# Two PSUM banks in one instruction: kept sums, residual additions and copies of a decoder trunk

## The chip, the cores and the metric

The kernel runs on one core of a Trainium2 chip. The core has a matmul engine (TensorE, PE in the profile), a vector engine (VectorE, DVE), an activation engine (ScalarE, ACT), a general engine (GpSimd, POOL) and a queue that issues transfers (SyncE, SP). Matmul results go to PSUM, eight banks of 512 float32 values in each of 128 partitions; VectorE and ScalarE read them from there. The metric is the device time of one execution in microseconds, as the median of several runs.

## The reference

A trunk of two layers works on 512 tokens of width 1024 in float32. Each layer is a half-step SwiGLU FFN, a token mixer and a second half-step FFN, each followed by a residual addition and a LayerNorm:

```
x = layer_norm(ALPHA * x + 0.5 * swiglu(x, w_gu, w_down), g, b)
x = layer_norm(ALPHA * x + mixer(x), g, b)
x = layer_norm(ALPHA * x + 0.5 * swiglu(x, w_gu, w_down), g, b)
swiglu(x) = (silu(x @ w_gate) * (x @ w_up)) @ w_down
```

The mixer of the first layer is block-sparse attention with eight heads, that of the second a causal pooling mixer. The hidden width of an FFN is 2816, so the four FFNs hold most of the matmul work.

## The kernel before

**Precision.** Every float32 operand is split into a rounded high part and the remainder (`split`, line 98): ScalarE copies the source into the rounded type, VectorE subtracts. A product is three matmuls that add into one bank (`mm3`, line 103: lines 105, 106 and 107).

**Seven products for eight.** The FFN's large products, and the value projection of the attention, are computed by a scheme of Strassen's kind: a 2 by 2 block product takes seven block products, numbered 1 to 7, instead of eight. Some products share an accumulator and go on adding into it: 1, 6, 7 and 4 add one after the other into one pair of banks, 2 into a second pair, 5 and 3 into that second pair after it has been read (`BANKS`, line 628). A product covers two row tiles, t=0 and t=1, one bank each, so its result lies in a pair of neighbouring banks. `products` (line 779) runs 24 matmuls; in the last step the three matmuls of t=0 come first, then the three of t=1.

**What reads a product.** After products 1, 6 and 5 `keep` (line 668) copies the partial sum to SBUF on ScalarE. After products 2, 7 and 3 `finish` (line 673) adds a kept sum to the accumulator on VectorE, then applies SiLU on ScalarE and multiplies on VectorE (`gate`, line 661). After product 4 the gate reads the accumulator directly. In the down projection `down_product` (line 810) adds each accumulator into the residual `ax` on VectorE (line 818). The attention's value projection has the same structure (`v_product`, line 928, with `keep`, `added` and `value`).

**Banks.** `bank(i, name)` (line 95) allocates a tile of one bank under the tag of bank i, so that a new tile on it waits for the readers of the old one. `SUMS` and `SECOND` (lines 633 and 634) say which pair a product uses; FFN 0 shifts all numbers by four. The outputs of `gate` are transposed on TensorE into one of two single banks in turn, and ScalarE copies them to `hT` (`to_features`, line 688); this happens after products 5 and 4.

**Order.** TensorE's order is that of the program. `order(eight)` (line 172) writes the products (i, jj) of an FFN out by hand, where jj numbers groups of hidden columns; jj = FF and FF + 1 stand for the two groups of the down projection. For FFNs 2, 3 and 5 (numbered with the mixers as phases 0 to 5) it begins

```
(1, 1), (2, 1), (1, 2), (5, 1), (6, 1), (7, 1), (3, 1), (4, 1), ...
```

and for FFN 0 with (1, 1), (2, 1), (6, 1), (5, 1), (7, 1), (3, 1), (1, 2), (4, 1). The later groups run 2, 6, 5, 7, 3, then 1 of the next group, then 4. The other engines' instructions are ordered at build time by a planner that simulates when each is ready; all waits are placed from the reads and writes of tiles. Weights stream through 20 slots of SBUF, are split on ScalarE and VectorE some units ahead of their use (`prepare`, line 263), and free their slots when TensorE has used them. Each product takes two units.

Of the kernel before, what the change touches and what calls it, by code (L numbers as in the profile page):

```python
# [25 lines left out]
F32 = mybir.dt.float32  # L26
F32R = mybir.dt.float32r
AF = mybir.ActivationFunctionType
ALU = mybir.AluOpType
# [3 lines left out]
P = 128  # L33
S = 512
D = 1024
FF = 2816
# [4 lines left out]
ALPHA = (2 * DEPTH) ** 0.25  # L41
# [42 lines left out]
def trunk(ctx, tc, x_in, xt, rel_bias, ln_g, ln_b, w_gu, w_gq, w_dq, w_down, w_v, a_in, a_out, b_in, b_group, b_scale, b_out, onehot, out):  # L84
    nc = tc.nc
# [6 lines left out]
    ps = enter(tc.tile_pool(name="ps", bufs=1, space=PSUM))  # L92
    dram = enter(tc.tile_pool(name="dram", bufs=1, space=bass.MemoryType.DRAM))

    def bank(i, name):
        return ps.tile([P, 512], F32, tag=f"b{i}", name=name)

    def split(hi, lo, src):

        nc.scalar.activation(hi, src, AF.Copy)  # L100
        return nc.vector.tensor_tensor(lo, src, hi.bitcast(F32), op=ALU.subtract)  # L101

    def mm3(acc, sh, sl, mh, ml, first, last, shared=False):

        nc.tensor.matmul(acc, sh, ml, start=first, stop=False, skip_group_check=shared)  # L105
        nc.tensor.matmul(acc, sh, mh, start=False, stop=False, skip_group_check=shared)  # L106
        nc.tensor.matmul(acc, sl, mh, start=False, stop=last, skip_group_check=shared)  # L107
# [189 lines left out]
    def weights():  # L297
        taken[0] += 1
        while len(parts) < taken[0]:
            load_needed()  # L300
            prepare()
        return parts[taken[0] - 1]

    def retire(count=1):

        retired[0] += count
        run_ahead()


    ax = glob.tile([P, NT, D], F32, name="ax")  # L310
# [317 lines left out]
    BANKS = {1: 0, 6: 0, 7: 0, 4: 0, 2: 1, 5: 1, 3: 1}  # L628
# [4 lines left out]
    SUMS = {1: 0, 2: 4, 3: 0, 4: 4, FF: 0, 5: 4, 0: 0, FF + 1: 4}  # L633
    SECOND, TURNED = 2, 6
# [3 lines left out]
    def ffn(n, x, dest):  # L638
        with tc.tile_pool(name=f"ffn{n}", bufs=1) as fp:
            hT = [fp.tile([P, GROUP, S], F32, name=f"hT{n}")]  # L640
            later, kept, waiting, turn = {}, {}, [], [0]
            eight = n == 0
# [3 lines left out]
            def banks(b, count, name):  # L646
                return [bank((b + 4 * eight) % 8 + t, f"{name}_{t}") for t in range(count)]
# [13 lines left out]
            def gate(out, g, u, sign):  # L661
                nc.scalar.activation(out, g, AF.Silu, scale=sign)  # L662
                return nc.vector.scalar_tensor_tensor(out, u, sign, out, op0=ALU.mult, op1=ALU.mult)

            def gated(name):
                return fp.tile([P, 2, 256], F32, tag="gated", bufs=3, name=f"gated{n}_{name}")

            def keep(i, jj, acc):
                kept[i, jj] = fp.tile([P, 2, S], F32, tag=f"kept{BANKS[i]}", bufs=2 - BANKS[i], name=f"kept{n}_{jj}_{i}")
                for t in range(2):  # L670
                    nc.scalar.activation(kept[i, jj][:, t], acc[t], AF.Copy)  # L671

            def finish(i, jj, acc):

                half, h, k, sign = DONE[i]
                out = gated(f"{jj}_{i}")
                if k is None:
                    for t in range(2):
                        ins = gate(out[:, t], acc[t][:, 0:256], acc[t][:, 256:512], sign)
                else:  # L680
                    k = kept.pop((k, jj))
                    for t in range(2):
                        nc.vector.tensor_tensor(k[:, t], k[:, t], acc[t], op=ALU.add)  # L683
                    ins = gate(out, k[:, :, 0:256], k[:, :, 256:512], sign)
                waiting.append((out, 4 * jj - 4 + 2 * half, h))
                return ins
# [90 lines left out]
            accs = {}  # L777

            def products(i, jj, b, amid=lambda q: None):

                if i in (1, 2, 5):
                    accs[jj, BANKS[i]] = banks(SECOND if i != 1 else SUMS[0] if eight and jj == FF + 1 else SUMS[jj], 2, f"d{n}_{jj}_{i}")
                acc = accs[jj, BANKS[i]]
                for q in range(2):
                    wh, wl = weights()
                    for k in range(2):
                        c = slice(k * 512, (k + 1) * 512)
                        for t in range(2):
                            o = b[:, :, 2 * q + k, t * P:(t + 1) * P]
                            mm3(acc[t], o[:, 0], o[:, 1], wh[:, c], wl[:, c], q == 0 and k == 0 and i in (1, 2, 5),  # L790
                                q == 1 and k == 1 and i in (2, 3, 4), True)
                    amid(q)
                return acc
# [16 lines left out]
            def down_product(i, g):  # L810


                acc = products(i, FF + g, hid[g].parts[i])
                for t0, d, sign in {1: ((0, 0, 1),), 2: ((0, 0, 1),), 6: ((2, 0, 1),), 5: ((2, 1, -1),), 7: ((2, 1, -1),),
                                    3: ((2, 0, 1),), 4: ((0, 1, -1),)}[i]:
                    for t in range(2):
                        r = ax[:, t0 + t, d * 512:(d + 1) * 512]
                        nc.vector.scalar_tensor_tensor(r, acc[t], 0.5 / ALPHA * sign, r, op0=ALU.mult, op1=ALU.add)  # L818
                if i in ((1, 2, 6, 5, 7) if g == 0 else (1, 2, 6, 5)):
                    next(operands)  # L820
                with tc.issue_after(hid[g].last.ins) if g == 0 and i in (2,) else ExitStack():
                    retire(2)

            for i, jj in ORDERS[not eight]:
# [11 lines left out]
                if n == 0 and (i, jj) in RESIDUAL:  # L836
                    with tc.issue_after(queued["load"].ins):
                        t = RESIDUAL.index((i, jj))
# [12 lines left out]
                if not eight and (i, jj) in ((1, 1), (2, 1)):  # L851
                    acc = products(i, jj, x.parts[i], head(i, jj))
                else:
                    acc = products(i, jj, x.parts[i])
                if i in (1, 6, 5):
                    keep(i, jj, acc)
                if i in DONE:
                    ins = finish(i, jj, acc)
# [35 lines left out]
    def attention(n, x, dest):  # L894
        held[0] = 4
        with tc.tile_pool(name="att", bufs=1) as ap:
            oT, qk, v, probs, pT = {}, {}, {}, {}, {}
# [8 lines left out]
            accs, kept = {}, {}  # L906

            def keep(i, acc):
                kept[i] = ap.tile([P, 2, 512], F32, tag=f"kept{i % 5}", name=f"vkept{i}")
                for t in range(2):  # L910
                    nc.scalar.activation(kept[i][:, t], acc[t], AF.Copy)

            def value(t, d, src, sign):
                hi, lo = v["hi"][:, t, d * 512:(d + 1) * 512], v["lo", t // 2][:, t % 2, d * 512:(d + 1) * 512]
                if sign == 1:
                    split(hi, lo, src)
                else:
                    nc.scalar.activation(hi, src, AF.Copy, scale=-1.0)
                    nc.vector.scalar_tensor_tensor(lo, src, -1.0, hi.bitcast(F32), op0=ALU.mult, op1=ALU.subtract)

            def added(i, acc):

                k = kept.pop(i)
                for t in range(2):
                    nc.vector.tensor_tensor(k[:, t], k[:, t], acc[t], op=ALU.add)
                return [k[:, t] for t in range(2)]

            def v_product(i):
                if i in (1, 2, 5):
                    accs[BANKS[i]] = [bank({1: 0, 2: 2, 5: 2}[i] + t, f"v{i}_{t}") for t in range(2)]  # L930
                acc = accs[BANKS[i]]
                for q in range(2):
                    wh, wl = weights()
                    for k in range(2):
                        c = slice(k * 512, (k + 1) * 512)
                        for t in range(2):
                            mm3(acc[t], *x.stationary(i, 2 * q + k, t), wh[:, c], wl[:, c], q == 0 and k == 0 and i in (1, 2, 5),
                                q == 1 and k == 1 and i in (2, 3, 4), True)
                if i == 2:
                    v["hi"] = lnp.tile([P, NT, D], F32R, tag="stage", name="vh")  # L940
                if i in (2, 7):
                    v["lo", len(v) - 1] = glob.tile([P, 2, D], F32R, tag="act", bufs=ACT, name=f"vl{len(v) - 1}")
                if i in (1, 6, 5):
                    keep(i, acc)
                else:
                    srcs = acc if i == 4 else added({2: 1, 7: 5, 3: 6}[i], acc)
                    t0, d, sign = {2: (0, 0, 1), 7: (2, 1, -1), 3: (2, 0, 1), 4: (0, 1, -1)}[i]
                    for t in range(2):
                        value(t0 + t, d, srcs[t], sign)
                with tc.issue_after(x.last.ins):  # L950
                    retire(2)

# [51 lines left out]
            for hp in range(H // 2):  # L1004
# [20 lines left out]
                else:  # L1025
                    for i in range(4):
                        acc = bank(i + 2 if hp == 1 and i < 2 else i % 2, f"qk{hp}_{i}")
                        a_block(x, acc, *blocks[i])
                        project(acc, *names[i])
                        if i == 1:  # L1030
                            ins = outputs(h - 2, 4 if hp == 1 else 0)
# [196 lines left out]
```

## Time and profile before

| | |
|---|---|
| median of 3 runs | 1667.8 us (1667.7 to 1668.12) |
| profiled execution, first to last instruction (span) | 1665.5 us |
| TensorE, matmuls | 1652.6 us busy, 99% |
| TensorE, weight loads | 1395.9 us, 84% |
| VectorE | 1340.2 us, 80%, 1766 instructions |
| ScalarE | 931.5 us, 56%, 1299 instructions |
| keeps, line 671 | 120 of one bank, 598 ns each |
| sums, line 683 | 120 of one bank, 680 ns each |
| residual additions, line 818 | 112 of one bank, 684 ns each |

The profile gives the profiled execution's time only as its span; 2.3 us lie between the span and the median. Matmuls overlap one another in the record: each shows 0.39 us, and they start 0.23 us apart. A row of waits reads "engine, tile, line <- engine, tile, line that it waited for: total us, times, longest". In a timeline, x2 joins two instructions that follow one another.

### The profile page before, as it was taken

To read this page: it belongs to the slowest core of one execution; us is meant where nothing else is said; L and a number is where in the kernel's file an instruction comes from. 1 tells how busy PE (TensorE), PEld (TensorE's weight loads), DVE (VectorE), ACT (ScalarE), POOL (GpSimd) and SP (SyncE) were. 2 spreads that over 40 slices of the span, in tenths; PEclk is the share of its full clock that TensorE was granted. 3 is DMA by queue.
4 is the path that set the end of the run, shared out by engine and by line. 5 is a ranking of instruction groups with operands and counts; after the bars stand their busy time and mean duration, and the time that the engine had idled before them with its cause. 6 is when DMAs were issued, how large, how long until landed. Compare 5 with 4: busy or idle time off the path is not lost.

```text
span 1665.5 us, 21722 instructions
## 1 busy us (share of the span) xinstructions
PE 1652.6 (99%) x8123; PEld 1395.9 (84%) x8123; DVE 1340.2 (80%) x1766; ACT 931.5 (56%) x1299; POOL 151.0 (9%) x196
## 2 busy tenths in 40 slices
PE   9999999999999999999999999999999999999997
PEld 8888888898888888888988888889898888888886
DVE  8778798798675888888868888888787698879696
ACT  6556556366445765555566655555453665656560
POOL 1101010000001011100010111100000201101000
PEclk9999999999999999999999999999999999999999
DMA  9778676805157488776685887666624878867641
GB/s 303 189 219 247 183 193 174 236 5 189 52 143 194 119 245 220 193 189 179 173 232 136 245 221 192 188 179 174 204 77 113 197 204 221 227 166 202 172 148 60
DMA packets 93579, 299.91 MB, mean 180 GB/s; under 512 B 9441, under 2 KB 22793, under 8 KB 93473
## 3 DMA queue, kind: packets, MB, share of 16 engines
q1 hardware_dynamic: 69600, 211.84, 37.0%
q0 software_dynamic: 23872, 86.68, 28.6%
q8 instruction: 64, 1.05, 0.2%
q14 instruction: 43, 0.34, 0.1%
HBM read 296.36 MB, written 4.74 MB: 181 GB/s over the span
## 4 chain that ended last, share of the span: by engine, by line
PE 98%; DVE 1%; ACT 0%; DMA 0%; SPq 0%; issue 0%; DVEq 0%; ACTq 0%
PE d L105 21%; PE d L107 21%; PE d L106 21%; PE acc L107 4%; PE acc L106 4%; PE acc L105 4%; PE ft L696 2%; PE qk L106 2%; PE qk L105 2%; PE qk L107 2%; PE gu L107 2%; PE gu L105 2%; PE gu L106 2%; PE tp L428 1%; PE u L106 1%; PE u L107 1%
## 5 line engine op out<-in xcount | busy, mean ns | idle before, releaser
L101 DVE TENSOR_TENSOR lo<-raw,hi 128x1024 fp32r<-128x1024 f32 (+1 forms) x476 | 572.1, 1216 | 121.2 <-ACT hi L100 95.9
L100 ACT ACTIVATE hi<-raw 128x1024 fp32r<-128x1024 f32 (+1 forms) x476 | 495.8, 1055 | 265.3 <-DVE lo L101 86.2
L105 PE MATMUL d<-lo,x 128*128 128x512 f32 x1080 | 423.8, 392 | 0.0
L107 PE MATMUL d<-hi,x 128*128 128x512 f32 x1080 | 420.9, 390 | 0.0
L106 PE MATMUL d<-hi,x 128*128 128x512 f32 x1080 | 420.4, 389 | 0.0
L105 PEld LDWEIGHTS d<-lo,x 128*128 128x128 f32 x1080 | 202.8, 188 | 43.1 <-ACT kept L671 1.3
L107 PEld LDWEIGHTS d<-hi,x 128*128 128x128 f32 x1080 | 202.7, 188 | 42.7
L106 PEld LDWEIGHTS d<-hi,x 128*128 128x128 f32 x1080 | 202.9, 188 | 40.9
L105 PE MATMUL d<-lo,xh 128*128 128x512 f32 x448 | 175.3, 391 | 0.0
L107 PE MATMUL d<-hi,xh 128*128 128x512 f32 x448 | 174.4, 389 | 0.0
L106 PE MATMUL d<-hi,xh 128*128 128x512 f32 x448 | 174.4, 389 | 0.0
L146 DVE TENSOR_TENSOR raw<-raw,raw 128x1024 f32<-128x1024 f32 x98 | 118.7, 1218 | 25.3 <-DMA raw<-in_ffn_w_dq 13.5
L253 POOL DMA_DIRECT2D raw<-in_ffn_w_gq x80 | 71.1, 893 | 684.6 <-DMA raw<-in_ffn_w_gq 171.3
L671 ACT ACTIVATE kept<-d 128x512 f32<-128x512 f32 x120 | 71.5, 598 | 68.3 <-PE d L107 65.4
L107 PEld LDWEIGHTS d<-hi,xh 128*128 128x128 f32 x448 | 84.1, 188 | 17.7
L106 PEld LDWEIGHTS d<-hi,xh 128*128 128x128 f32 x448 | 84.1, 188 | 17.2
L105 PEld LDWEIGHTS d<-lo,xh 128*128 128x128 f32 x448 | 84.1, 188 | 16.9
L818 DVE SCALAR_TENSOR_TENSOR ax<-d,ax 128x512 f32<-128x512 f32 x112 | 73.3, 684 | 14.4 <-PE d L107 14.3
L683 DVE TENSOR_TENSOR kept<-kept,d 128x512 f32<-128x512 f32 x120 | 78.1, 680 | 6.5 <-PE d L107 6.4
L662 ACT ACTIVATE gated<-kept 128x512 f32<-128x512 f32 x60 | 37.8, 630 | 72.9 <-DVE kept L683 72.2
L460 DVE SCALAR_TENSOR_TENSOR ax<-acc,ax 128x512 f32<-128x512 f32 x48 | 33.0, 687 | 52.8 <-PE acc L107 52.3
L105 PE MATMUL acc<-lo,h 128*128 128x512 f32 x192 | 75.2, 392 | 0.0
(199 smaller groups left out, 2664.4 us busy)
## 6 DMA issues: line engine op xcount, KB each, us to landing
raw<-in_ffn_w_gq SPq DMA_DIRECT2D x206, 512.0 KB, 4.8
raw<-in_ffn_w_gq POOLq DMA_DIRECT2D x80, 512.0 KB, 7.4
raw<-in_ffn_w_dq SPq DMA_DIRECT2D x80, 512.0 KB, 3.4
raw<-in_ffn_w_dq POOLq DMA_DIRECT2D x32, 512.0 KB, 6.4
raw<-in_ffn_w_down SPq DMA_DIRECT2D x24, 512.0 KB, 4.3
ax<-in_ln_b POOLq DMA_DIRECT2D x20, 512.0 KB, 8.4
raw<-in_ffn_w_gu SPq DMA_DIRECT2D x18, 512.0 KB, 4.7
raw<-in_a_w_in SPq DMA_DIRECT2D x16, 512.0 KB, 4.8
```

What stands on the lines that cost most here:

```text
L100: nc.scalar.activation(hi, src, AF.Copy)
L101: return nc.vector.tensor_tensor(lo, src, hi.bitcast(F32), op=ALU.subtract)
L105: nc.tensor.matmul(acc, sh, ml, start=first, stop=False, skip_group_check=shared)
L106: nc.tensor.matmul(acc, sh, mh, start=False, stop=False, skip_group_check=shared)
L107: nc.tensor.matmul(acc, sl, mh, start=False, stop=last, skip_group_check=shared)
L146: nc.vector.tensor_tensor(d, d, more, op=ALU.add)
L253: queued["acc"] = nc.gpsimd.dma_start(p.tile, p.plus, accum_op=ALU.add)
L662: nc.scalar.activation(out, g, AF.Silu, scale=sign)
L671: nc.scalar.activation(kept[i, jj][:, t], acc[t], AF.Copy)
L683: nc.vector.tensor_tensor(k[:, t], k[:, t], acc[t], op=ALU.add)
L696: nc.tensor.transpose(tp[:, c, t * P:(t + 1) * P], out[:, t, c * P:(c + 1) * P], ident)
L818: nc.vector.scalar_tensor_tensor(r, acc[t], 0.5 / ALPHA * sign, r, op0=ALU.mult, op1=ALU.add)
```

## The change

All eight banks become one tile, `banks8`. `bank(i, name)` returns a slice of it, and the new `bank_pair(i)` a slice of two neighbouring banks. `products` and `v_product` take their accumulators as such a pair; the matmuls still write one bank each, in the same order. Each loop over t=0 and t=1 that read the two banks with an instruction each becomes one instruction over both: the keeps, the sums of a kept part and an accumulator, the direct gate of product 4, the residual additions, and in the attention the keeps, the sums and the splits of the values.

```diff
+    banks8 = ps.tile([P, 8, 512], F32, name="banks8")
+
     def bank(i, name):
-        return ps.tile([P, 512], F32, tag=f"b{i}", name=name)
+        return banks8[:, i]
+
+    def bank_pair(i):
+        return banks8[:, i:i + 2]
...
             def keep(i, jj, acc):
                 kept[i, jj] = fp.tile([P, 2, S], F32, tag=f"kept{BANKS[i]}", bufs=2 - BANKS[i], name=f"kept{n}_{jj}_{i}")
-                for t in range(2):
-                    nc.scalar.activation(kept[i, jj][:, t], acc[t], AF.Copy)
+                nc.scalar.activation(kept[i, jj], acc, AF.Copy)
...
                 if k is None:
-                    for t in range(2):
-                        ins = gate(out[:, t], acc[t][:, 0:256], acc[t][:, 256:512], sign)
+                    ins = gate(out, acc[:, :, 0:256], acc[:, :, 256:512], sign)
                 else:
                     k = kept.pop((k, jj))
-                    for t in range(2):
-                        nc.vector.tensor_tensor(k[:, t], k[:, t], acc[t], op=ALU.add)
+                    nc.vector.tensor_tensor(k, k, acc, op=ALU.add)
...
-                    accs[jj, BANKS[i]] = banks(SECOND if i != 1 else SUMS[0] if eight and jj == FF + 1 else SUMS[jj], 2, f"d{n}_{jj}_{i}")
+                    accs[jj, BANKS[i]] = bank_pair(((SECOND if i != 1 else SUMS[0] if eight and jj == FF + 1 else SUMS[jj]) + 4 * eight) % 8)
...
-                    for t in range(2):
-                        r = ax[:, t0 + t, d * 512:(d + 1) * 512]
-                        nc.vector.scalar_tensor_tensor(r, acc[t], 0.5 / ALPHA * sign, r, op0=ALU.mult, op1=ALU.add)
+                    r = ax[:, t0:t0 + 2, d * 512:(d + 1) * 512]
+                    nc.vector.scalar_tensor_tensor(r, acc, 0.5 / ALPHA * sign, r, op0=ALU.mult, op1=ALU.add)
...
             def value(t, d, src, sign):
-                hi, lo = v["hi"][:, t, d * 512:(d + 1) * 512], v["lo", t // 2][:, t % 2, d * 512:(d + 1) * 512]
+                hi, lo = v["hi"][:, t:t + 2, d * 512:(d + 1) * 512], v["lo", t // 2][:, :, d * 512:(d + 1) * 512]
...
-                for t in range(2):
-                    nc.vector.tensor_tensor(k[:, t], k[:, t], acc[t], op=ALU.add)
-                return [k[:, t] for t in range(2)]
+                nc.vector.tensor_tensor(k, k, acc, op=ALU.add)
+                return k
...
-                    for t in range(2):
-                        value(t0 + t, d, srcs[t], sign)
+                    value(t0, d, srcs, sign)
```

More of the change, by code (lines that the diff above doesn't have):

```diff
@@ L789, in products @@
                             o = b[:, :, 2 * q + k, t * P:(t + 1) * P]
-                            mm3(acc[t], o[:, 0], o[:, 1], wh[:, c], wl[:, c], q == 0 and k == 0 and i in (1, 2, 5),
+                            mm3(acc[:, t], o[:, 0], o[:, 1], wh[:, c], wl[:, c], q == 0 and k == 0 and i in (1, 2, 5),
                                 q == 1 and k == 1 and i in (2, 3, 4), True)
@@ L909, in keep @@
                 kept[i] = ap.tile([P, 2, 512], F32, tag=f"kept{i % 5}", name=f"vkept{i}")
-                for t in range(2):
-                    nc.scalar.activation(kept[i][:, t], acc[t], AF.Copy)
+                nc.scalar.activation(kept[i], acc, AF.Copy)
             def value(t, d, src, sign):
-                hi, lo = v["hi"][:, t, d * 512:(d + 1) * 512], v["lo", t // 2][:, t % 2, d * 512:(d + 1) * 512]
+                hi, lo = v["hi"][:, t:t + 2, d * 512:(d + 1) * 512], v["lo", t // 2][:, :, d * 512:(d + 1) * 512]
                 if sign == 1:
@@ L923, in added @@
                 k = kept.pop(i)
-                for t in range(2):
-                    nc.vector.tensor_tensor(k[:, t], k[:, t], acc[t], op=ALU.add)
-                return [k[:, t] for t in range(2)]
+                nc.vector.tensor_tensor(k, k, acc, op=ALU.add)
+                return k
             def v_product(i):
                 if i in (1, 2, 5):
-                    accs[BANKS[i]] = [bank({1: 0, 2: 2, 5: 2}[i] + t, f"v{i}_{t}") for t in range(2)]
+                    accs[BANKS[i]] = bank_pair({1: 0, 2: 2, 5: 2}[i])
                 acc = accs[BANKS[i]]
@@ L936, in v_product @@
                         for t in range(2):
-                            mm3(acc[t], *x.stationary(i, 2 * q + k, t), wh[:, c], wl[:, c], q == 0 and k == 0 and i in (1, 2, 5),
+                            mm3(acc[:, t], *x.stationary(i, 2 * q + k, t), wh[:, c], wl[:, c], q == 0 and k == 0 and i in (1, 2, 5),
                                 q == 1 and k == 1 and i in (2, 3, 4), True)
@@ L947, in v_product @@
                     t0, d, sign = {2: (0, 0, 1), 7: (2, 1, -1), 3: (2, 0, 1), 4: (0, 1, -1)}[i]
-                    for t in range(2):
-                        value(t0 + t, d, srcs[t], sign)
+                    value(t0, d, srcs, sign)
                 with tc.issue_after(x.last.ins):
```

## The prediction

> **What bounds the kernel now.** I read the head of the page first, then the chain of waits, then the busy time of each engine by stage.
>
> ```profile
> span 1665.5 us, 21722 instructions
> PE 1652.6 (99%) x8123; PEld 1395.9 (84%) x8123; DVE 1340.2 (80%) x1766; ACT 931.5 (56%) x1299; POOL 151.0 (9%) x196
> PE 98%; DVE 1%; ACT 0%; DMA 0%; SPq 0%; issue 0%; DVEq 0%; ACTq 0%
> 0.00:10.50 10.50, 8.12 (x50) 7.50 (x50) 4.14 (x6) 5.91 (x7) 0.70 (x6) 1.00 0.79 288
> 1656.00:1666.00 10.00, 0.69 (x4) 0.22 (x2) 5.09 (x12) 0.20 (x1) 0.00 (x0) 0.68 0.28 107
> sum 1645.50, PE 1643.79 PEld 1388.15 DVE 1330.97 ACT 925.37 POOL 150.26; mean PE 328.76 PEld 277.63 DVE 266.19 ACT 185.07 POOL 30.05
> ```
>
> The first row of the two stages is the start-up, the second the tail (last residual add, LayerNorm, output). The sum row covers the five stages between, 10.5 to 1656 us. There TensorE is idle for 1645.50 − 1643.79 = 1.71 us in all. The rest of its idle time is start-up and tail, which the change does not touch. So VectorE's 80% and ScalarE's 56% bound nothing: relief for them is worth something only where TensorE waits for them. Those waits are listed by the weight loads, which run ahead of the matmuls and stop first:
>
> ```profile
> PEld ft L696 <- ACT hT L697: 1.6, 3, 0.5
> PEld d L105 <- ACT kept L671: 1.3, 3, 0.4
> PEld d L105 <- DVE raw L146: 0.9, 1, 0.9
> PEld o L105 <- DVE pr L971: 0.9, 1, 0.9
> PEld pt L983 <- DVE pr L975: 0.5, 1, 0.5
> PEld qk L105 <- DVE oT L101: 0.2, 1, 0.2
> ```
>
> Columns: total us, times, longest. Everything that could be won in the middle is 5.4 us, if all six rows went to nothing. Only the first two have an instruction of the change in or in front of them. They come three times each, once in each of the last three FFNs, so the question is what the change does at those two places.
>
> **The change part by part.** Prices of the instructions, from the groups with shapes kept apart:
>
> ```profile
> L671 ACT ACTIVATE kept<-d 128x512 f32<-128x512 f32 x120 | 71.5, 598 | 68.3 <-PE d L107 65.4
> L683 DVE TENSOR_TENSOR kept<-kept,d 128x512 f32<-128x512 f32 x120 | 78.1, 680 | 6.5 <-PE d L107 6.4
> L818 DVE SCALAR_TENSOR_TENSOR ax<-d,ax 128x512 f32<-128x512 f32 x112 | 73.3, 684 | 14.4 <-PE d L107 14.3
> L100 ACT ACTIVATE hi<-raw 128x1024 fp32r<-128x1024 f32 x474 | 494.5, 1057 | 264.4 <-DVE lo L101 86.2 <-PE d L105 62.9 <-PE d L107 43.0
> L100 ACT ACTIVATE pT<-pl 128x512 fp32r<-128x512 f32 x8 | 5.0, 631 | 5.7 <-DVE pl L1076 5.6
> L146 DVE TENSOR_TENSOR raw<-raw,raw 128x1024 f32<-128x1024 f32 x98 | 118.7, 1218 | 25.3 <-DMA raw<-in_ffn_w_dq 13.5 <-DMA raw<-in_ffn_w_gq 11.4
> ```
>
> The trace has no two-bank read. On ScalarE 512 more elements cost 1057 − 631 = 426 ns, so a pair copy is 598 + 426 = 1.02 us. Lower bound: 0.60 us, one bank's copy, if both banks streamed at once. Upper bound: 1.28 us, what two copies take together now (timeline below). I take 1.02, since the slope is from the same engine and operation at the same size. On VectorE the nearest 1024-element row is 1.22 us; two halves are 1.36.
>
> Busy time removed: ScalarE 60 × (2 × 0.598 − 1.02) = 10.4 us in the FFN keeps; VectorE 60 × (2 × 0.680 − 1.22) + 56 × (2 × 0.684 − 1.22) = 16.7 us in the sums and residual additions. The twenty direct gates and the attention's three keeps, three sums and four value splits shed an instruction per pair in the same way. All of it lies beside TensorE's work, so I cost the gain at nothing. No DMA is added, removed or moved in the program text.
>
> What the change adds is a later start. The first copy of a pair now starts when the t=0 group of matmuls is done, while the t=1 group runs. The pair copy waits for both, and both banks are given back at its end. The place where that hurts is product (6,1) followed at once by (7,1), which adds into the same two banks; `order(False)` puts them next to each other in FFNs 2, 3 and 5:
>
> ```profile
> 585.18 0.39 PE L107 MATMUL d<-hi,x 128*128 128x512 f32 x1
> 585.61 1.28 ACT L671 ACTIVATE kept<-d 128x512 f32<-128x512 f32 x2 [0.37 <-PE d L107]
> 585.87 0.39 PE L107 MATMUL d<-hi,x 128*128 128x512 f32 x1
> 586.26 0.19 PEld L105 LDWEIGHTS d<-lo,x 128*128 128x128 f32 x1 [0.43 <-ACT kept L671]
> 586.27 0.50 PE L105 MATMUL d<-lo,x 128*128 128x512 f32 x1
> 590.10 1.06 ACT L100 ACTIVATE x<-st 128x1024 fp32r<-128x1024 f32 x1 [3.20 <-DVE st L370]
> ```
>
> Now: t=0 ends at 585.18 + 0.39 = 585.57, its copy starts 0.04 later and ends at 585.61 + 0.60 = 586.21, and TensorE goes on at 586.26. After: t=1 ends at 586.26, the pair copy runs from 586.30 to 587.32, and TensorE goes on at 587.37. That is 0.04 + 1.02 + 0.05 = 1.11 us later than now, with bounds 0.69 and 1.37 by the two prices. Behind the waiting matmul stands the whole of TensorE's queue. ScalarE has nothing to put in between: its next work starts at 590.10. Three times: **+3.3 us** (2.1 to 4.1).
>
> The second place is the third group of transposes after (5,2), which needs the bank that the first `hT` copy empties; that copy stands behind the keep on ScalarE:
>
> ```profile
> 616.58 1.06 ACT L100 ACTIVATE hi<-raw 128x1024 fp32r<-128x1024 f32 x1 [0.72 <-PE d L105]
> 619.07 1.29 ACT L671 ACTIVATE kept<-d 128x512 f32<-128x512 f32 x2 [1.43 <-PE d L107]
> 619.33 0.40 PE L107 MATMUL d<-hi,x 128*128 128x512 f32 x1
> 620.26 1.08 ACT L697 ACTIVATE hT<-ft 128x512 f32<-128x512 f32 x2
> 620.90 0.42 PEld L696 LDWEIGHTS ft<-ident,gated 128*128 128x128 f32 x4 [0.54 <-ACT hT L697]
> ```
>
> Now the keeps end at 619.07 + 1.29 = 620.36. After, the pair starts at 619.33 + 0.40 + 0.04 = 619.77 and ends at 620.79: 0.43 later, and `hT` and the transposes with it (bounds 0 and 0.69). Three times: **+1.3 us** (0 to 2.1).
>
> Everywhere else a whole product lies between a pair's last matmul and the next one on its banks: 24 matmuls at (585.87 − 585.18) / 3 = 0.23 us, so 5.5 us. The pair ends 0.4 to 0.55 us later than the second half does now when the engine was waiting for it, and slightly earlier when the engine is behind. The tightest places now:
>
> ```profile
> 38.99 0.58 ACT L671 ACTIVATE kept<-d 128x512 f32<-128x512 f32 x1
> 41.47 0.39 PE L105 MATMUL d<-lo,x 128*128 128x512 f32 x1
> 599.80 1.27 DVE L683 TENSOR_TENSOR kept<-kept,d 128x512 f32<-128x512 f32 x2
> 603.10 0.48 PE L105 MATMUL d<-lo,x 128*128 128x512 f32 x1
> ```
>
> The first pair is the keep of (1,1) in FFN 0, done at 39.57 and needed at 41.47; the second the sum of (3,1) in FFN 2, done at 601.07 and needed at 603.10. Slacks of 1.9 and 2.0 us hide a half microsecond. If the cover went, each would cost what is left over it.
>
> Sum: 3.3 + 1.3 = 4.6 us (2.1 to 6.2). The span goes from 1665.5 to 1670.1. The profiled execution's span is 2.3 us under the median of the timed runs, 1667.8, which I take as what lies around the span; it stays. So 1672.4 us, with 1669.9 and 1674.0 from the bounds.
>
> The Trainium skill, Perfetto Trace Analysis, Optimizing Scalar/DVE Operations, says that grouping into larger operations helps where the engine is saturated, and that where Scalar and Vector are not saturated but leave bubbles on other engines, breaking instructions up may let work finish sooner. By its first half, with VectorE at 80% taken as saturated, the time would fall by at most the 5.4 us of waits; by its second half it rises as summed above. The rows of waits bear out the second.
>
> **The rivals.** *The planner fills the longer gap.* ScalarE idles 1.43 us before the keep of (5,2) and would idle 0.7 more. Weight slots come free twice a product, every 2.7 us; the copy at 616.58 waited for one, so the next could be ready at 619.3, before the pair. A copy of 1.06 us there ends at 620.36, the pair with the present overlap of 0.1 at about 621.3 instead of 620.79: 0.5 more, three times, 1673.9. For it: in FFN 0 the second copy of (1,1) at 38.99 already stands behind something else. Against: today the second keep, not such a copy, runs at that place.
>
> *Only the first wait grows.* If the planner sets the `hT` copies so that they do not stand behind the pair, the second place keeps its price: 1667.8 + 3.3 = 1671.1. Against: they are ready only after transposes that follow the product's last matmul, when the pair is ready already.
>
> *The other side: TensorE's own wait instructions.*
>
> ```profile
> L105 PEldq EVENT_SEMAPHORE  x74: 51/51/51, 4.8 to 1614.4; - x74
> L696 PEldq EVENT_SEMAPHORE  x43: 51/51/51, 48.3 to 1564.0; - x43
> ```
>
> TensorE's queue has 117 separate waits of 51 ns, 6.0 us. One tile and one reader per pair could make them needless. If they lay on the path and all went, the time would be 1667.8 − 6.0 + 4.6 = 1666.4; it decides only once more than three quarters go. Against: 6.0 us does not fit into 1.71 us of idle time, so most are hidden already.
>
> *The change does not do what it says*: each two-bank instruction is run bank by bank with its own wait, 1667.8. Nothing in the trace speaks for it. *One tile is waited for as a whole*: each of the 196 evacuations (60 + 60 + 20 + 56) holds TensorE about 1.1 us, 1667.8 + 216 = 1884. Against: the slices are of separate banks.
>
> **How the numbers follow.** Forecast 0.58, gap filled 0.12, only the first wait 0.14, wait instructions 0.06, no effect 0.07, whole tile 0.03. About 0.2%, 3.3 us, is what a measurement of this kernel can tell from no change. Of the forecast's 0.58 I put 0.11 under that bound, for its low price; of the second wait's rival 0.10 of 0.14, as 1671.1 is on the bound. Slower: 0.47 + 0.12 + 0.04 + 0.03 = 0.66. Faster: 0.03 of the wait instructions and 0.01 of no effect, 0.04. Same: 0.30. The range, 1667.5 to 1674.5, takes in both bounds, the first two rivals and no effect.
>
> **What would show it.** The keep should be 60 instructions of 128x1024 at about 1.02 us; the wait of L105 for the keep three times about 1.5 us instead of 0.43; the wait of L696 for `hT` three times about 0.97 instead of 0.54; TensorE's middle idle about 6.3 us instead of 1.7. ScalarE and VectorE should show less busy time and the time should not follow. A wait of TensorE at a third place, or a two-bank copy far from 1.02, would prove a step wrong; a median under 1667.8 all of it.

## The result, and the profile after

The changed kernel takes 1676.57 us (median of 5 runs, 1675.48 to 1676.7), beside 1667.78 us for the kernel before on the same chip: a ratio of 1.0051, 95% interval [1.004, 1.0063]. It is slower by 8.8 us. The forecast was 1672.4 us, 4.6 us more than before, with a range of 1667.5 to 1674.5. The profiled execution has a span of 1673.7 us, 8.2 us more than before.

The head of the page after, its chain of waits, the groups with shapes kept apart, and the stage between start-up and tail:

```profile
span 1673.7 us, 21430 instructions
PE 1654.1 (99%) x8123; PEld 1397.0 (83%) x8123; DVE 1328.2 (79%) x1623; ACT 922.7 (55%) x1212; POOL 150.8 (9%) x196
PE 94%; DVE 3%; ACT 2%; DMA 1%; issue 0%; SPq 0%; DVEq 0%; ACTq 0%
L675 ACT ACTIVATE kept<-banks 128x1024 f32<-128x1024 f32 x60 | 61.0, 1017 | 46.6 <-PE banks L112 46.5
L685 DVE TENSOR_TENSOR kept<-kept,banks 128x1024 f32<-128x1024 f32 x60 | 72.9, 1214 | 4.1 <-PE banks L112 4.1
L819 DVE SCALAR_TENSOR_TENSOR ax<-banks,ax 128x1024 f32<-128x1024 f32 x56 | 68.2, 1218 | 18.1 <-PE banks L112 17.2
10.50:1664.00 1653.50, 1644.16 (x8070) 1387.94 (x8071) 1318.81 (x1607) 916.81 (x1205) 150.10 (x190) 1.00 0.66 179
```

There are 292 instructions fewer (21722 before), VectorE is busy 12.0 us less and ScalarE 8.8 us less, and the time went up. TensorE's share of the chain fell from 98% to 94%: VectorE (3%) and ScalarE (2%) now stand in it. In the middle TensorE is idle for 1653.50 − 1644.16 = 9.3 us instead of 1.7. The weight loads' waits say where (total us, times, longest):

```profile
PEld banks L110 <- ACT kept L675: 4.6, 3, 1.5
PEld banks L698 <- ACT hT L699: 4.3, 3, 1.4
PEld banks L110 <- DVE lo L106: 2.6, 3, 0.9
```

Lines have moved by some: L110, L111 and L112 are the three matmuls that were L105 to L107, L105 and L106 the split that was L100 and L101, L675 the keep, L685 the sum, L698 and L699 the transposes and `hT`. The first two rows stood before with 1.3 and 1.6 us. The third is new. Each comes once in FFNs 2, 3 and 5; here they are in FFN 2.

**Place 1, (6,1) to (7,1)**, timeline after:

```profile
586.78 0.39 PE L112 MATMUL banks<-hi,x 128*128 128x512 f32 x1
587.20 1.02 ACT L675 ACTIVATE kept<-banks 128x1024 f32<-128x1024 f32 x1 [0.50 <-PE banks L112]
588.28 0.19 PEld L110 LDWEIGHTS banks<-lo,x 128*128 128x128 f32 x1 [1.54 <-ACT kept L675]
588.28 0.50 PE L110 MATMUL banks<-lo,x 128*128 128x512 f32 x1 [1.11 <-ACT kept L675]
```

From the last matmul of (6,1) to the first of (7,1), start to start, 588.28 − 586.78 = 1.50 us; before, 586.27 − 585.87 = 0.40. So +1.10 us, against 1.11 forecast.

**Place 2, the third transposes after (5,2)**, timeline after:

```profile
621.30 1.06 ACT L105 ACTIVATE hi<-raw 128x1024 fp32r<-128x1024 f32 x1 [3.01 <-PE banks L110]
621.33 0.40 PE L112 MATMUL banks<-hi,x 128*128 128x512 f32 x1
622.27 1.00 ACT L675 ACTIVATE kept<-banks 128x1024 f32<-128x1024 f32 x1
623.17 1.07 ACT L699 ACTIVATE hT<-banks 128x512 f32<-128x512 f32 x2
623.81 0.42 PEld L698 LDWEIGHTS banks<-ident,gated 128*128 128x128 f32 x4 [1.45 <-ACT hT L699]
```

The matmuls of (5,2) end at 621.33 + 0.40 = 621.73, and the pair could have started then. But ScalarE had begun another weight's split copy (its half of `split`, line 105 here) at 621.30, so the keep starts at 622.27 and `hT` behind it. The wait is 1.45 us instead of 0.54: +0.91, where 0.43 was forecast.

**Place 3, in the middle of a product, 8 us after the sum of (2,1)**. VectorE before, then VectorE and TensorE after:

```profile
568.86 1.30 DVE L683 TENSOR_TENSOR kept<-kept,d 128x512 f32<-128x512 f32 x2 [0.45 <-PE d L107]
570.08 1.22 DVE L101 TENSOR_TENSOR x<-st,x 128x1024 fp32r<-128x1024 f32 x1
571.21 1.22 DVE L101 TENSOR_TENSOR lo<-raw,hi 128x1024 fp32r<-128x1024 f32 x1
...
574.09 1.22 DVE L101 TENSOR_TENSOR lo<-raw,hi 128x1024 fp32r<-128x1024 f32 x1
```

```profile
569.52 1.22 DVE L106 TENSOR_TENSOR x<-st,x 128x1024 fp32r<-128x1024 f32 x1 [1.13 <-ACT x L105]
570.66 1.21 DVE L685 TENSOR_TENSOR kept<-kept,banks 128x1024 f32<-128x1024 f32 x1
571.79 1.22 DVE L375 SCALAR_TENSOR_TENSOR st<-st 128x1024 f32<-128x1024 f32 x1
572.93 1.22 DVE L106 TENSOR_TENSOR lo<-raw,hi 128x1024 fp32r<-128x1024 f32 x1
...
574.67 1.21 DVE L157 TENSOR_TENSOR raw<-raw,raw 128x1024 f32<-128x1024 f32 x1
575.81 1.22 DVE L106 TENSOR_TENSOR x<-st,x 128x1024 fp32r<-128x1024 f32 x1
576.94 2.35 DVE L106 TENSOR_TENSOR lo<-raw,hi 128x1024 fp32r<-128x1024 f32 x2
...
577.38 0.39 PE L112 MATMUL banks<-hi,x 128*128 128x512 f32 x1
578.21 0.50 PE L110 MATMUL banks<-lo,x 128*128 128x512 f32 x1 [0.45 <-DVE lo L106]
578.55 0.39 PE L111 MATMUL banks<-hi,x 128*128 128x512 f32 x1
```

Before, VectorE took the first half of the sum as soon as t=0 was done, then the second half, then the split of the operand `x`. After, the pair sum comes behind that split, and two more instructions (`raw` and the next `x`) have moved ahead of the second `lo`, which starts at 576.94 instead of 574.09. It is the remainder of a weight, done at 576.94 + 1.22 = 578.16, which TensorE needs at 577.38 + 0.23 = 577.61. From 577.38 to 578.21 are 0.83 us instead of 0.23, and the matmul after it is 0.11 late too: +0.71.

Per FFN 1.10 + 0.91 + 0.71 = 2.72 us; three times 8.2 us, the whole difference of the spans. The starts of the 8123 matmuls, set side by side in the two traces, drift apart at these nine places and by 0.2 us at the start-up; no other step exceeds 0.1 us.

### The profile page after: what moved, and what is told of

It is laid out like the page before. It is cut to its first block, busy times and chain, and to the rows that moved or that the text cites. A ratio compares the mean times of both kernels' runs of the same rounds, so it can differ in the third digit from the quotient of the medians.

```text
span 1673.7 us, 21430 instructions
## 1 busy us (share of the span) xinstructions
PE 1654.1 (99%) x8123; PEld 1397.0 (83%) x8123; DVE 1328.2 (79%) x1623; ACT 922.7 (55%) x1212; POOL 150.8 (9%) x196
## 4 chain that ended last, share of the span: by engine, by line
PE 94%; DVE 3%; ACT 2%; DMA 1%; issue 0%; SPq 0%; DVEq 0%; ACTq 0%
PE banks L110 30%; PE banks L112 30%; PE banks L111 30%; PE banks L698 2%; PE banks L433 1%; ACT st L441 1%; DVE lo L106 1%; ACT kept L675 1%; DVE x L106 0%; PE banks L981 0%; DVE st L375 0%; ACT x L105 0%; DMA raw<-in_ffn_w_gu 0%; ACT hi L105 0%; DVE kept L685 0%
## 5 line engine op out<-in xcount | busy, mean ns | idle before, releaser
L106 DVE TENSOR_TENSOR lo<-raw,hi 128x1024 fp32r<-128x1024 f32 (+1 forms) x476 | 570.4, 1216 | 130.3 <-ACT hi L105 101.2
L105 ACT ACTIVATE hi<-raw 128x1024 fp32r<-128x1024 f32 (+1 forms) x476 | 495.2, 1056 | 306.3 <-PE banks L110 103.0
L110 PE MATMUL banks<-lo,x 128*128 128x512 f32 x1136 | 446.0, 393 | 4.7 <-ACT kept L675 3.3
L112 PE MATMUL banks<-hi,x 128*128 128x512 f32 x1136 | 442.7, 390 | 0.0
L111 PE MATMUL banks<-hi,x 128*128 128x512 f32 x1136 | 442.2, 389 | 0.0
L110 PEld LDWEIGHTS banks<-lo,x 128*128 128x128 f32 x1136 | 213.3, 188 | 51.1 <-ACT kept L675 4.6
L112 PEld LDWEIGHTS banks<-hi,x 128*128 128x128 f32 x1136 | 213.2, 188 | 44.6
L111 PEld LDWEIGHTS banks<-hi,x 128*128 128x128 f32 x1136 | 213.4, 188 | 43.0
L110 PE MATMUL banks<-lo,xh 128*128 128x512 f32 x448 | 175.3, 391 | 0.0
L112 PE MATMUL banks<-hi,xh 128*128 128x512 f32 x448 | 174.4, 389 | 0.0
L111 PE MATMUL banks<-hi,xh 128*128 128x512 f32 x448 | 174.4, 389 | 0.0
L112 PE MATMUL banks<-x,lo 128*128 128x256 f32 (+1 forms) x424 | 133.8, 316 | 0.8 <-DVE lo L106 0.8
L110 PE MATMUL banks<-x,hi 128*128 128x256 f32 (+1 forms) x424 | 134.3, 317 | 0.0
L111 PE MATMUL banks<-x,hi 128*128 128x256 f32 (+1 forms) x424 | 133.6, 315 | 0.0
L112 PEld LDWEIGHTS banks<-hi,xh 128*128 128x128 f32 x448 | 84.1, 188 | 17.6
L110 PEld LDWEIGHTS banks<-lo,xh 128*128 128x128 f32 x448 | 84.1, 188 | 17.1
L111 PEld LDWEIGHTS banks<-hi,xh 128*128 128x128 f32 x448 | 84.2, 188 | 17.1
L675 ACT ACTIVATE kept<-banks 128x1024 f32<-128x1024 f32 x60 | 61.0, 1017 | 46.6 <-PE banks L112 46.5
L112 PEld LDWEIGHTS banks<-x,lo 128*128 128x128 f32 x424 | 80.8, 190 | 6.2 <-DVE lo L106 1.2
L110 PEld LDWEIGHTS banks<-x,hi 128*128 128x128 f32 x424 | 80.9, 191 | 5.5 <-DVE oT L106 0.2
```

The source lines that it names most:

```text
L675: nc.scalar.activation(kept[i, jj], acc, AF.Copy)
```

## The experiments

All times are beside runs of the kernel before on the same chip, whose median was 1667.51, 1667.69, 1667.5 and 1667.3 us in the four groups of runs below. This table is the result of all of them in one view. The columns in the middle are what the three places cost per FFN over the kernel before, read off the matmuls of FFN 2 in each run's trace as above (FFNs 3 and 5 agree within 0.1 us); "sum" is three times their total; the last columns are measured.

| run | place 1 | place 2 | place 3 | sum | measured | ratio to before, interval |
|---|---|---|---|---|---|---|
| the changed kernel | 1.10 | 0.91 | 0.71 | +8.2 | +8.8 | 1.0051 [1.004, 1.0063] |
| e1, one tile, all by bank | 0 | 0 | 0 | 0 | +0.2 | 1.0002 [0.9993, 1.0011] |
| e21, pair (6,1) alone | 1.10 | 0 | 0 | +3.3 | +3.2 | 1.0019 [1.001, 1.0029] |
| e22, pair (5,2) alone | 0 | 0.43 | 0 | +1.3 | +1.0 | 1.0008 [0.9998, 1.0017] |
| e32, pairs (6,1), (5,2) | 1.10 | 0.43 | 0 | +4.6 | +4.8 | 1.003 [1.0018, 1.0042] |
| e2, all keeps, nothing else | 1.10 | 0.91 | 0.29 | +6.9 | +6.5 | 1.0038 [1.0023, 1.0053] |
| e3, all but the keeps | 0.80 | 0 | 0 | +2.4 | +2.6 | 1.0015 [1.0005, 1.0025] |
| e4, all but keep (6,1) | 0.80 | 0.91 | 0.71 | +7.3 | +7.7 | 1.0046 [1.0031, 1.0061] |
| e13, all but keep (1,1) | 1.10 | 0.91 | 0 | +6.0 | +5.8 | 1.0034 [1.0021, 1.0047] |
| e25, keep (1,1) and the sums | 0.80 | 0 | 0.71 | +4.5 | +4.8 | 1.0031 [1.0019, 1.0042] |
| e23, pair (1,1) alone | 0.80 | 0 | 0.29 | +3.3 | +3.2 | 1.0019 [1.001, 1.0028] |
| e30, pairs (1,1), (6,1) | 1.10 | 0.74 | 0.29 | +6.4 | +6.0 | 1.0037 [1.0025, 1.005] |
| e31, pairs (1,1), (6,1), (5,2) | 1.10 | 0.91 | 0.29 | +6.9 | +6.5 | 1.0041 [1.0028, 1.0053] |
| e7, the changed kernel, order held at (5,2) | 1.10 | 0.43 | 0.71 | +6.7 | +6.8 | 1.0041 [1.0028, 1.0053] |
| e19, three keeps by bank, order held | 0.80 | 0 | 0 | +2.4 | +2.0 | 1.0013 [1.0004, 1.0022] |
| e20, e19 and another bank | 0.80 | −0.50 | 0 | +0.9 | +0.7 | 1.0006 [0.9997, 1.0015] |
| e9, kernel before and another bank | 0 | −0.50 | 0 | −1.5 | −1.1 | 0.9993 [0.9984, 1.0002] |

The sums stand within 0.6 us of every measurement. Nothing else in the change has a price that can be seen beyond that.

**The parts (e1, e2, e3).** e1 has the one tile and no pair at all; e2 pairs only the keeps of the FFNs; e3 pairs all but these.

```diff
 e1 (the keeps; sums, gates, residual additions and the attention likewise)
-                nc.scalar.activation(kept[i, jj], acc, AF.Copy)
+                for t in range(2):
+                    nc.scalar.activation(kept[i, jj][:, t], acc[:, t], AF.Copy)
 e2: as e1, with this line as in the changed kernel
 e3: the changed kernel, with these two lines
```

> The changed kernel with all its two-bank instructions taken apart again: only the one tile of eight banks is left. Theory (the later start of the pair copies costs all of it): 1667.8 us, within 0.5, with TensorE's waits as before the change (0.43 three times for the keep, 0.54 three times for hT). Rival (one tile makes the waits coarser): up to the changed kernel's 1675 to 1677.

> Of the two-bank instructions only the FFN's sixty keeps on ScalarE are left; sums, gates, residual additions and the attention go bank by bank. Theory (the keeps cost all): 1675.5 to 1676.6, with the three waits of the changed kernel, 1.53 for the keep, 1.45 for hT and 0.87 for a weight split, three times each. Rival (the pairs on VectorE cost part): below 1674, the wait for the weight split gone, 3.3 + 2.8 = 6.1 over the kernel before at most.

> The changed kernel with only the FFN's keeps taken apart again; all pairs on VectorE and in the attention stay. Theory: 1667.8 within 0.5, waits as before. Rival (pairs on VectorE cost part): 1669.9, with the 2.1 us of waits for the weight split left.

Measured 1667.68, 1674.0 and 1670.09 us. The tile itself costs nothing that can be measured: in e1 the two waits are those of the kernel before, within 0.1 us.

```profile
PEld banks L701 <- ACT hT L702: 1.6, 3, 0.5
PEld banks L110 <- ACT kept L676: 1.4, 4, 0.4
```

It also took away 40 of the 117 separate waits of TensorE that the prediction counted (74 and 43; now 70 and 7), and the time did not fall:

```profile
L110 PEldq EVENT_SEMAPHORE  x70: 51/51/51, 4.8 to 1614.5; - x70
L701 PEldq EVENT_SEMAPHORE  x7: 51/51/51, 48.3 to 1386.2; - x7
```

e2 landed between the two expectations: the keeps alone make most of the loss, but place 3 is smaller there (0.29), so the pairs on VectorE add to it (e25 below has 0.71 with the sums as pairs, e23 0.29 without). e3 was a miss: with every keep by bank nothing should have been lost, and 2.6 us were. Its ScalarE at place 1:

```profile
585.78 0.60 ACT L676 ACTIVATE kept<-banks 128x512 f32<-128x512 f32 x1 [0.94 <-PE banks L112]
586.28 1.05 ACT L105 ACTIVATE hi<-raw 128x1024 fp32r<-128x1024 f32 x1
587.23 0.59 ACT L676 ACTIVATE kept<-banks 128x512 f32<-128x512 f32 x1
```

and its waits:

```profile
PEld banks L110 <- ACT kept L676: 4.2, 6, 0.9
```

A split copy now stands between the two copies of (6,1), and TensorE waits six times instead of three. No pair is on ScalarE at this place. Pairs elsewhere had changed the order of its work.

**The two forecast terms by themselves (e21, e22, e32).** From e1, one or two keeps of FFNs 2, 3 and 5 are made a pair; the order at the three places stays that of the kernel before. VectorE's order is the same throughout; on ScalarE nothing moves in e22, and in e21 and e32 one split copy moves earlier by one place (at about 615 us in FFN 2), at no cost.

```diff
-                for t in range(2):
+                for t in (slice(0, 1), slice(1, 2)) if eight or (i, jj) not in ((6, 1), (5, 2)) else (slice(0, 2),):
                     nc.scalar.activation(kept[i, jj][:, t], acc[:, t], AF.Copy)
 e32 as shown; e21 with (6, 1) alone, e22 with (5, 2) alone
```

> One tile, everything bank by bank, but the keep of product (6,1) in FFNs 2, 3 and 5 as one pair copy. At this place the planner sets the other engines' instructions in the order of the kernel before. Theory (the later start alone costs 1.11 us here): the wait of L110 for the keep is about 1.53 three times, nothing else changes, 1667.6 + 3.3 = 1670.9. Rival (the later start is made up for elsewhere, and the first run's loss comes of the order alone): under 1669.2.

> One tile, everything bank by bank, but the keep of product (5,2) in FFNs 2, 3 and 5 as one pair copy; here too the planner leaves the order as before, with one split copy ahead of the keep and one behind hT. Theory (of the 0.92 us that the third transposes lost in the changed kernel, 0.43 are the pair's later end and the rest the second split copy that was set ahead of it): the wait for hT is 0.97, 1667.6 + 1.3 = 1668.9. Rival (the pair alone costs it all): wait 1.45, 1667.6 + 2.8 = 1670.4.

> One tile, everything by bank, and only the keeps of (6,1) and (5,2) in FFNs 2, 3 and 5 as pairs: six instructions fewer than by bank. VectorE's order after (2,1) and ScalarE's at (6,1) and (5,2) stay as before the change. Theory (the prediction's two terms hold where the order stays): waits of 1.5 and 0.97 us, three times each, 1667.7 + 3.3 + 1.3 = 1672.3. Rival (the two delays overlap, or the pair of (5,2) alone draws a split copy ahead): under 1671.3 or over 1673.3.

Measured 1670.85, 1668.69 and 1672.11 us. The waits of e32:

```profile
PEld banks L110 <- ACT kept L676: 4.6, 3, 1.5
PEld banks L701 <- ACT hT L702: 2.9, 3, 1.0
```

These are the forecast's waits of 1.5 and 0.97 us, and 1672.11 is 0.3 us from the forecast's time, 1672.4. Its two terms were right, singly and together, as long as the order of the other engines stays. (e22 alone can't be told from no change by its interval; its wait can.)

**Undoing one pair, or adding others (e4, e13, e25).**

```diff
 e4
-                nc.scalar.activation(kept[i, jj], acc, AF.Copy)
+                for t in (slice(0, 1), slice(1, 2)) if not eight and (i, jj) == (6, 1) else (slice(0, 2),):
+                    nc.scalar.activation(kept[i, jj][:, t], acc[:, t], AF.Copy)
 e13: the same with (1, 1)
 e25: e1 with the keep of (1, 1) a pair, and the sums of the FFNs as in the changed kernel
```

> The changed kernel with one keep taken apart, that of product (6,1) in FFNs 2, 3 and 5. Theory (each of the three places has its own price): the wait of L110 for the keep falls from 1.53 to 0.43, the other two stay, 3.3 us under the changed kernel, 1672.2 to 1673.3. Rival (what is lost at one place is won back or lost at the next): less than 1.5 us under the changed kernel.

> The changed kernel with one keep taken apart, that of product (1,1) in FFNs 2, 3 and 5; the sum of (2,1) stays a pair. Theory (that keep starts the reordering on VectorE): the wait for a weight split, 0.87 three times, is gone, the other two stay, 2.1 us under the changed kernel, about 1673.8. Rival (the pair sum on VectorE does it by itself): the wait stays, 1675.5 to 1676.6.

> One tile, bank by bank, but the keep of product (1,1) in FFNs 2, 3 and 5 and all sums on VectorE as pairs. The planner sets VectorE's work after (2,1) as in the changed kernel: the split of an operand ahead of the sum, the weight splits behind. Theory (third place: keep of (1,1) and sum of (2,1) together): the wait of L110 for a weight split comes back, 0.87 three times, 2.1 us; a split copy between the two copies of (6,1) costs another 2.0 as in the kernel with the keeps by bank; 1671.7 in all. Rival (the third place needs another pair): no wait for a weight split, 1669.6.

Measured 1675.19, 1673.53 and 1672.49 us. e4 missed: the pair of (6,1) was undone, but the split copy of e3 slipped between its two copies, and 0.80 of the 1.10 us stayed. e13 was right: without the pair of (1,1) place 3 is gone. e25 brought it back in full, with no other keep paired.

**Order alone (e23, e30, e31).** (1,1) is a keep for which TensorE waits in no run, so by the prediction it is free. It is the only pair of e23. e30 adds (6,1), e31 (5,2) too.

```diff
-                for t in range(2):
+                for t in (slice(0, 1), slice(1, 2)) if eight or (i, jj) not in ((1, 1), (6, 1)) else (slice(0, 2),):
 e30 as shown; e31 with (5, 2) as well, e23 with (1, 1) alone
```

> Only the keep of (1,1) as a pair, for which TensorE never waits. In the program as built an operand split stands between the two sums after (2,1), and a split copy between the two copies of (6,1). Theory (order alone costs): 0.8 us three times at (6,1) and 0.2 after (2,1), 2.4 + 0.6 = 3.0, so 1670.7. Rival (a pair whose banks are not needed soon is hidden, as the prediction had it): 1667.7.

> Only the keeps of (1,1) and (6,1) as pairs, that of (5,2) by bank. In the program as built a split copy stands between the two copies of (5,2). Theory (the order, not the pair at the place, makes the second place dearer): the hT copies stand behind first copy, split copy and second copy, about 0.74 us later than before, so 3.3 + 2.2 + 0.6 after (2,1) = 6.1 over the kernel before, 1673.8. Rival (without the pair of (5,2) the wait for hT stays 0.54): 1671.6.

> As the run before this one, with the keep of (1,1) a pair as well: three of 60 kinds of keep, nine instructions fewer. In the program as built a split copy stands ahead of the pair of (5,2), and an operand split between the two sums after (2,1). Theory: 3.3 + 3 x 0.92 at (5,2) + about 0.6 after (2,1) = 6.7 over the kernel before, 1674.4, as with all 60 keeps paired. Rival (the other 51 keeps matter too): 1672.3 to 1673.

Measured 1670.52, 1673.35 and 1673.78 us: 3.2, 6.0 and 6.5 us over the kernel before, where the theory had 3.0, 6.1 and 6.7. VectorE in e23:

```profile
569.18 0.69 DVE L688 TENSOR_TENSOR kept<-kept,banks 128x512 f32<-128x512 f32 x1 [0.64 <-PE banks L112]
569.79 1.22 DVE L106 TENSOR_TENSOR x<-st,x 128x1024 fp32r<-128x1024 f32 x1
570.92 0.68 DVE L688 TENSOR_TENSOR kept<-kept,banks 128x512 f32<-128x512 f32 x1
```

One pair on ScalarE, some 6 us earlier, and the operand split has gone between the two halves of the sum. That moves the weights' remainders at place 3, and a split copy at place 1: 3.2 us, none of it a wait for the pair. In e30 the keep of (5,2) is by bank as before the change, and place 2 is dearer all the same:

```profile
620.29 0.60 ACT L676 ACTIVATE kept<-banks 128x512 f32<-128x512 f32 x1 [2.16 <-PE banks L112]
620.78 1.05 ACT L105 ACTIVATE hi<-raw 128x1024 fp32r<-128x1024 f32 x1
621.73 0.59 ACT L676 ACTIVATE kept<-banks 128x512 f32<-128x512 f32 x1
622.21 1.09 ACT L702 ACTIVATE hT<-banks 128x512 f32<-128x512 f32 x2
```

and the wait for `hT`, 3.8 / 3 = 1.27 us against 0.54 before:

```profile
PEld banks L701 <- ACT hT L702: 3.8, 3, 1.3
```

Three pairs in each of FFNs 2, 3 and 5 (e31) cost what all sixty keeps cost (e2).

**Holding the order, and another bank (e7, e19, e20, e9).** e7 is the changed kernel with the second split copy after (5,2) issued behind the pair. e19 takes the three keeps by bank and holds the split copies behind them; e20 and e9 give the third transposes after (5,2) bank 0, e20 on top of e19, e9 on the kernel before. (`copied` is the keep's instruction. The three keeps by bank are 9 instructions more, 18 in all.)

```diff
 e7
+                elif not eight and (i, jj) == (5, 2):
+                    retire()
+                    with tc.issue_after(copied.ins):
+                        retire()
 e19: the same, the keeps of (1, 1), (6, 1) and (5, 2) by bank, and
-                        with tc.issue_after(x.last.ins):
+                        with tc.issue_after(x.last.ins), tc.issue_after(copied.ins) if i == 6 else ExitStack():
 e9, e20
+                    third = not eight and i == 5 and len(waiting) == 0 and jj == 2
-                    tp = banks(TURNED + turn[0] % 2, 1, f"ft{n}_{f}_{h}")[0].rearrange("p (c s) -> p c s", c=2)
+                    tp = banks(0 if third else TURNED + turn[0] % 2, 1, f"ft{n}_{f}_{h}")[0].rearrange("p (c s) -> p c s", c=2)
```

> The changed kernel with one ordering added: after product (5,2) in FFNs 2, 3 and 5 the second split copy of the next weights is issued behind the pair's keep instead of ahead of it. Nothing else differs. Theory (of the second place's price, 0.92 us against 0.43 forecast, 0.5 comes from that copy standing ahead of the pair): the wait for hT falls from 1.46 to 0.97 us three times, so 1.5 us less than the changed kernel, about 1675.1 against 1676.6. Rival (the transposes are late for another reason): no change, 1676.6.

> The changed kernel with the keeps of products (1,1), (5,2) and (6,1) in FFNs 2, 3 and 5 taken by bank again (two instructions each, 18 more in all), and with the split copies that the planner had let overtake them held behind the second copy of (6,1) and of (5,2). The other 51 keeps, all sums, gates and residual additions stay in pairs. Theory (the loss is those three places and the order around them, and pairs cost nothing elsewhere): no wait longer than before the change, 1667.8. Rival (pairs also cost by something that no wait shows, or the planner reorders at yet another place): 1669 or more.

> The kernel of the run before this one (three keeps by bank, copies held behind them, pairs elsewhere), and the third transposes after (5,2) in bank 0. Theory: 1667.8 less the 0.54 us of that wait three times, 1666.2, level with the kernel before with the third bank alone; pairs add no gain of their own, since nothing waits for VectorE or ScalarE elsewhere. Rival (the 20 us less busy time of the two engines are worth something once the waits are gone): under 1665.5.

> The kernel before with one edit: the third group of transposes after product (5,2) in FFNs 2, 3 and 5 uses bank 0, which has been read at that point, instead of the bank that the first hT copy still empties. Theory (the 0.54 us wait for hT is wholly a wait for that bank): it goes, 3 x 0.54 = 1.6 us, so 1666.2 and a ratio of 0.999 to the kernel before. Rival (bank 0 is needed again soon, or the transposes or the next product wait for something else as late): 1667.7, no change.

Measured 1674.33, 1669.52, 1668.16 and 1666.39 us. In e7 ScalarE waits for the matmuls and takes the pair first:

```profile
621.95 1.02 ACT L675 ACTIVATE kept<-banks 128x1024 f32<-128x1024 f32 x1 [3.48 <-PE banks L112]
622.87 1.08 ACT L699 ACTIVATE hT<-banks 128x512 f32<-128x512 f32 x2
```

Its wait for `hT`:

```profile
PEld banks L698 <- ACT hT L699: 2.9, 3, 1.0
```

The wait falls from 1.45 to 0.97 us (2.9 / 3), so the copy ahead was the other half of place 2's price. e19 missed by 2 us: place 2 and place 3 are free, but at (6,1) a split copy still runs between the two copies, as in e3. The order that I added holds only the copies issued after (6,1) in the program, and this is not one of them: in e1 ScalarE ran it ahead of both. e20 sits on the same 0.80. In e9 the wait for `hT` is gone from the list (TensorE is 0.50 us earlier behind it) and 1.1 us of the time; its interval reaches to 1.0002, so it can't be told from the kernel before. None of these kernels clearly beats it.

## Why the prediction was right or wrong

- **Nothing to win: right.** VectorE and ScalarE lost 20.8 us of busy time and TensorE got none of it. No effect falls by the sign, whole-tile waits (+216 us) by the size. TensorE's own wait instructions fall by e1: 40 of the 117 are gone there, and the ratio is 1.0002 [0.9993, 1.0011]; the other 77 stayed, so what they would give is not shown.
- **Prices: right.** The pair copy took 1.017 us (1.02 forecast), the sum 1.214 and the residual addition 1.218 (1.22). VectorE saved 12.0 us instead of 16.7 and more, because two halves that follow one another overlap in the record (1.30 us for two, not 1.36). ScalarE's keeps saved 71.5 − 61.0 = 10.5 us; the forecast's own terms give 10.6, not the 10.4 that it states. Nothing hung on either.
- **Place 1: right**, 1.10 against 1.11, by itself in e21. "ScalarE has nothing to put in between" held here, but not in general: in e3, e4, e19, e20, e23 and e25 a split copy runs between the two copies, for 0.80 us.
- **Place 2: mis-sized**, 0.91 against 0.43. The 0.43 is right where the order stays (e22, e32). The rest is the rival "the planner fills the longer gap": 0.5 more, as it was priced, at the place it named. I gave it 0.12, because "today the second keep, not such a copy, runs at that place". That was the old order, taken as evidence for the new one. Nor does the longer gap bring the copy there: e22 has the same pair and not the copy, e30 the copy and not the pair. The pairs of (1,1) and (6,1) were enough for it in e30; in the changed kernel the second of them is copied at 587.20 us, 34 us before the split copy at 621.30.
- **"Everywhere else … slacks of 1.9 and 2.0 us hide a half microsecond": the step that failed.** It asked only when the banks come back, and for that the slack does hide it. It left the order of ScalarE and VectorE as it was, as a term of nothing and without a reason. In the kernels as built another instruction can stand ahead of the merged one or between two halves, and the work that is pushed back can be a weight's remainder (place 3), the second copy of another keep (place 1 in e23) or the pair itself (place 2). e23 prices this alone at 3.2 us with one such keep. In the changed kernel it is place 3 (2.1 us) and the dearer part of place 2 (1.4 us), together the difference between 4.6 and the span's 8.2. The measured 8.8 is 0.6 more; the profiled execution was the fastest of the five (1675.48 us), so its trace need not show all of it.
- The Trainium skill, Perfetto Trace Analysis, Optimizing Scalar/DVE Operations, says that where Scalar and Vector are not saturated but cause bubbles on other engines, breaking instructions up may let work finish sooner. The trace agrees, in the other direction: VectorE was busy 80% and ScalarE 56%, and larger instructions made the bubbles on TensorE, 9.3 us instead of 1.7.

Open: what sets the order at place 2. Its dearer part also comes in e4, with only (6,1) by bank, and in e13, with only (1,1) by bank, so with the rest paired neither of the two is needed. In every run that puts the split copy there, VectorE's weight sums and remainders before it (604 to 616 us in FFN 2) stand in another order as well; of the other runs only e7 has that order, and there the edit holds the copy. Which leads to which is not shown. That the planner reorders because the pair is ready later by its own simulated clock is argued, not shown: that clock was not read.

## What to carry to other kernels

Here one copy out of two accumulators instead of two delayed the first by the time of the second's matmuls (0.69 us) and gave both back at its end: price it at the place where the accumulator, or what queues behind the copy, is needed at once. Where a planner orders the engines, price every edit twice: with the old order, and with the nearest ready instruction put ahead. Slack on a buffer covers only the first: one merged copy in each of three FFNs, for which TensorE never waited, changed the order of other work for some 25 us behind it and cost 3.2 us in all, as much as the dearest direct wait (3.3).
